# Moving split-matrix sums and modulation-gate sums between the stages of a hybrid attention and mLSTM layer

## The chip, the cores and the metric

The kernel runs on one core of a Trainium2 chip. The metric is device time in microseconds (us) of one execution; times of several executions are given as their median. The engines are TensorE (PE), VectorE (DVE), ScalarE (ACT) and GpSimd (POOL); each works through its own queue in order. SyncE (SP) issues most DMAs, POOL and ACT issue a few. A profile is taken of one execution.

## The reference, cut to what matters

One layer, 256 tokens of width 1024, float32. The input is normalised and modulated by a vector `c`, projected by one wide matrix `w_in` into thirteen parts, sent through a block attention (8 heads) and a chunked mLSTM (4 heads), and the two branches are gated, added and projected out.

```python
ada = c @ w_ada + b_ada
shift, scale, gate = split(ada, 3)
h = rmsnorm(x, norm_w) * (1 + scale) + shift
qa, ka, va, za, qm, km, vm, zm, om, ig, fg, ga, gm = split(h @ w_in)
ya = (attention(rmsnorm(qa), rmsnorm(ka), va) * silu(za)) @ w_att_proj
qm, km = split(silu(causal_dwconv(concat(qm, km))))
hm = rmsnorm(sigmoid(om) * mlstm(qm, km, vm, ig, fg))
ym = (hm * silu(zm)) @ w_ml_proj
y = sigmoid(ga) * ya + sigmoid(gm) * ym
return x + gate * (y @ w_out)
```

`gate` is the last third of `c @ w_ada`: a vector of 1024, used only in the last line. Its weights are 4 MB.

## The kernel before, in words

Float32 products are made of rounded parts. Every matrix is split into a high part (rounded, by ACT: `wh`, line 449) and a low part (the rest, by DVE: `wl`, line 453), and a product is three matmuls: high by high, high by low, low by high. The activations after modulation are kept as `hTh` and `hTl`, transposed.

After a first phase (modulation, normalisation and the first columns of `w_in`, some 52 us) the work is a list of chunks of 512 columns: ka, va, za, qm, zm, km, att (attention projection), vm, ga, om, gm, ml (mixer projection) and out. Each chunk is four steps of PE, so steps are numbered through: za is 12 to 19, qm 20 to 27, zm 28 to 41, km 42 to 49, att 50 to 57, vm 58 to 71, ga 72 to 79, om 80 to 93, gm 94 to 101, ml 102 to 109, out from 110 on. The three chunks zm, vm and om have fourteen steps: they are done as one level of Strassen's scheme with seven products instead of eight. That needs sums of quarters of the weights (`sum_forms`, line 495: tiles t1 and t4 and sums in place, some by an accumulating DMA that POOL issues) and sums of quarters of the activations: `left_sums` (lines 500 to 503 and 510) makes four sums in the tile `lsum`, in two parts, and `left_split` (lines 516 and 517) rounds each on ACT into `Sh` and subtracts on DVE into `Sl`.

The order of everything is written out by hand. At step g the program issues, in this order: for zm, vm and om the evacuation of a finished product; the split of the weights that step g + 4 will use (there are five buffers for `wh` and `wl`); at the first step of a chunk the evacuation of the chunk before; then all hooks that were put at this step with `at(step, ...)`; the weight loads that have become free (six raw buffers); and last the matmuls of the step. `start(name)` is a chunk's first step, `done(name, half)` the one after its last. Each engine executes its share in that order. A hook put at a step thus stands on its engine's queue behind the split for four steps later and ahead of the split of the next step. Steps in the set `pool_lo` have their low part made by POOL instead of DVE; there are six, 26, 27, 49, 50, 53 and 54.

What the change touches:

- `left_sums` at steps 17 and 18, `left_split` at steps 20, 21, 23 and 26.
- The gate vector: `gate_init` brings `c` to all partitions (at step 23 into the third part of the first tile in slot s5, at step 78 again into a tile of its own). `gate_load(q)` loads a quarter of the gate weights, 1 MB, by SP. `gate_acc(j)` multiplies an eighth with `c` and sums it on DVE (line 936, eight of them). `gate_write` and `gate_read` bring the vector by way of DRAM to all partitions, and the output stage multiplies with it (line 956).
- Slots: large tiles share memory under names (s0 to s6, bias). A new tile in a slot waits for the last readers of the tile before. The gate quarters are in s4 (step 23), s5 (step 24), bias (step 88) and s0 (step 99). The tile of the gate vector itself is in s5. `lsum` is in bias, behind the attention's bias table, which the last scores read at step 16.
- `ga_mult` multiplies the sigmoid of ga with the attention branch (line 827), in two halves at steps 77 and 97.
- Around steps 94 to 101 the mLSTM ends: `ml_num` (the numerator, line 875 on DVE), `ml_y` (factors, three small operations on POOL among them, lines 889 to 891), `ml_y2` (scaling, line 900, DVE), `ml_T` (transposes on PE, line 911, then a rounded part `ymh` on ACT, line 915, and a low part `yml` on DVE, line 916). `yh` and `yl` for the output stage are made in `ev_ml` (lines 840 to 843).

Of the kernel before, what the change touches and what calls it, by code (L numbers as in the profile page):

```python
# [9 lines left out]
F32 = mybir.dt.float32  # L10
# [5 lines left out]
D = 1024  # L16
# [48 lines left out]
def tile_hybrid(ctx: ExitStack, tc: tile.TileContext, x, c, params, params2, rel_t, w_row, ada_mod, ada_gate,  # L65
# [136 lines left out]
    cb = ph.tile([128, D], F32, name="cb")  # L202
# [77 lines left out]
    for step in P1_STEPS:  # L280
        op, k = step[0], int(step[1])
# [42 lines left out]
    C, step0, owner = {}, [], []  # L324
# [8 lines left out]
    def start(name, half=0):  # L333
        return step0[C[name, half]]

    def done(name, half):
        return step0[C[name, half]] + (14 if name in STRASSEN else 4)
# [81 lines left out]
    def free(tag):  # L419
        if tag in FREE:  # L420
            hl.tile([128, FREE.pop(tag)], F32, name="free_" + tag, bufs=1)

    def slot(tag, shape, dt, name):
        free(tag)
        return hl.tile(shape, dt, name=name, tag=tag, bufs=1)
# [4 lines left out]
    whl = {}  # L430
    HB = 5
    pool_lo = set()
    for nm, hf in (("qm", 0), ("km", 0), ("km", 1)):
        s = done(nm, hf) + (2 if nm == "qm" else 3)
        pool_lo.update((s, s + 1))
# [22 lines left out]
    def at(step, fn, *a):  # L458
        hooks.setdefault(step, []).append((fn, a))
# [4 lines left out]
    T = {}  # L464
# [49 lines left out]
    def left_split(i):  # L514
        r = T["lsum"][:, (3, 0, 2, 1)[i]]
        nc.scalar.copy(T["Sh"][:, i], r)
        nc.vector.tensor_tensor(T["Sl"][:, i], r, T["Sh"][:, i].bitcast(F32), op=OP.subtract)

    def left(p, k):
# [400 lines left out]
    def gate_init(i):  # L920
        if i == 0:
            T["gcol"] = hl.tile([128, KT], F32, name="gcol")
            T["gw", 1] = slot("s5", [128, 3, D], F32, "gw")
            T["cb"] = T["gw", 1][:, 2]
        else:
            T["cb"] = hl.tile([128, D], F32, name="cbg", tag="NM", bufs=1)
        nc.scalar.dma_start(T["cb"], bass.AP(tensor=c.tensor, offset=c.offset, ap=[[0, 128], [1, D]]))

    def gate_load(q):
        if q != 1:  # L930
            T["gw", q] = slot(("s4", None, "bias", "s0")[q], [128, 2, D], F32, "gw")
        nc.sync.dma_start(T["gw", q][:, 0:2], ada_gate[:, 2 * q:2 * q + 2])

    def gate_acc(j):
# [7 lines left out]

    def gate_read():
        gd = T["gd"]
        T["gateb"] = slot("s5", [128, D], F32, "gateb")
        nc.sync.dma_start(T["gateb"], bass.AP(tensor=gd.tensor, offset=gd.offset, ap=[[0, 128], [1, D]]))

    def load_x():
# [52 lines left out]
    at(s + 4, ml_scores, 2)  # L1001
    at(s + 4, ml_scores, 3)
    at(start("qm") + 3, gate_init, 0)
    at(start("om") - 2, gate_init, 1)
    at(done("ga", 0) + 1, ga_mult, 0)
    at(start("gm") + 3, ga_mult, 1)
    for q, (nm, i, j, k) in enumerate((("qm", 3, 6, 7), ("qm", 4, 23, 25), ("gm", -6, 2, 5), ("ml", -3, 1, 3))):
        s = start(nm)
        at(s + i, gate_load, q)
        at(s + j, gate_acc, 2 * q)  # L1010
        at(s + k, gate_acc, 2 * q + 1)
    at(start("ml") + 5, gate_write)
    at(start("ml") + 7, gate_read)
    at(start("qm") - 3, left_sums, 0)
    at(start("qm") - 2, left_sums, 1)
    for i in range(4):
        at(start("qm") + (0, 1, 3, 6)[i], left_split, i)
    for nm in STRASSEN:
        s = start(nm)
        for p in (3, 4, 5):  # L1020
# [45 lines left out]
    for g in range(NG):  # L1066
# [36 lines left out]
        if ch["kind"] == "str":  # L1103
            p = kp // 2
            o = mmt[ci][(0, 2, 0, 1, 0, 2, 0)[p]]
            for kk in range(2):
                k = 2 * (kp % 2) + kk
# [5 lines left out]
        for kk in range(2):  # L1113
            k = 2 * kp + kk
# [75 lines left out]
```

## Time and profile before

| | |
|---|---|
| median of 3 runs | 358.18 us (357.94 to 358.29) |
| the profiled execution | 357.32 us, of it 355.5 us span |
| mean granted PE clock | 0.993 |
| PE busy | 345.3 us, 97% |
| DVE busy | 293.0 us, 82% |
| ACT busy | 236.4 us, 66% |
| POOL busy | 78.4 us, 22% |
| HBM read | 81.89 MB, 234 GB/s over the span |

Busy shares are means over the whole span. PE's busy time counts matmuls from a modelled start to a modelled end, so it is not a measure of how much work PE could still take; where it waits is seen in the timeline, in which each row gives the start, the length, the engine, the line, the operation, the tiles (written <- read), the shapes, and in brackets the idle time of the engine before it and who ended that.

### The profile page before, as it was taken

The page shows a single profiled execution, that of the slowest core. Times are in us where ns is not written, and L with a number is a line of the kernel's source. Part 1 is how long each engine was busy: PE and PEld are TensorE (multiplying, and loading weights), DVE is VectorE, ACT ScalarE, POOL GpSimd, SP SyncE. Part 2 cuts the span into 40 slices and gives each one's busy share as a digit, 9 for nine tenths or more (in the row PEclk, how much of TensorE's full clock was granted, in tenths as well). Part 3 has the DMA queues.
Part 4 walks back from the last instruction along what each step waited for, and adds up shares of the span by engine and source line. Part 5 has one row for each costly group of instructions (what it writes and reads, how often), then busy time and mean ns, then how long its engine had stood idle before and what let it go on. Part 6 is the DMA issues. An engine that isn't in the chain of part 4 may idle for free.

```text
span 355.5 us, 6025 instructions
## 1 busy us (share of the span) xinstructions
PE 345.3 (97%) x2308; PEld 315.4 (89%) x2308; DVE 293.0 (82%) x423; ACT 236.4 (66%) x366; POOL 78.4 (22%) x88
## 2 busy tenths in 40 slices
PE   8999999999999999799999999999999999999995
PEld 4988889888999999577999998899988998999885
DVE  4899986898958949999986888998988879698772
ACT  3777797989784895778664647884587744654410
POOL 4920004685004356000145250000100014000000
PEclk9999999999999999899999999999999999999998
DMA  8999999994666789956660892929959486065011
GB/s 292 418 418 420 414 372 359 223 269 183 238 207 216 119 307 362 214 206 267 220 254 5 271 287 37 365 104 320 270 167 393 147 278 261 2 235 180 0 61 59
DMA packets 29534, 83.72 MB, mean 235 GB/s; under 512 B 2109, under 2 KB 5185, under 8 KB 28994
## 3 DMA queue, kind: packets, MB, share of 16 engines
q1 hardware_dynamic: 26944, 78.08, 61.6%
q0 software_dynamic: 2112, 4.19, 6.9%
q10 hardware_dynamic: 450, 1.07, 0.9%
q8 instruction: 18, 0.29, 0.3%
q14 instruction: 10, 0.08, 0.1%
HBM read 81.89 MB, written 1.45 MB: 234 GB/s over the span
## 4 chain that ended last, share of the span: by engine, by line
PE 83%; DVE 11%; issue 3%; ACT 1%; DMA 0%; POOL 0%; POOLq 0%; DVEq 0%
PE mm L1127 12%; PE mm L1129 12%; PE mm L1130 12%; PE pm L186 9%; DVE wl L453 6%; PE aux L1109 4%; PE aux L1111 4%; PE aux L1110 4%; PE mm L1120 4%; PE mm L1122 4%; PE mm L1121 4%; PE pg L186 2%; PE xps L244 2%; DVE gw L936 1%; DVE qmT L787 1%
## 5 line engine op out<-in xcount | busy, mean ns | idle before, releaser
L453 DVE TENSOR_TENSOR wl<-raw,wh 128x1024 fp32r<-128x1024 f32 (+1 forms) x100 | 121.1, 1235 | 20.9 <-ACT wh L449 20.8
L449 ACT CAST wh<-raw 128x1024 fp32r<-128x1024 f32 (+1 forms) x106 | 107.2, 1031 | 21.0 <-PE mm L1129 18.4
L1127 PE MATMUL mm<-hTh,wh 128*128 128x256 f32 x320 | 90.4, 282 | 0.2 <-DVE qmT L787 0.2
L1130 PE MATMUL mm<-hTh,wl 128*128 128x256 f32 x320 | 89.5, 280 | 0.0
L1129 PE MATMUL mm<-hTl,wh 128*128 128x256 f32 x320 | 89.5, 280 | 0.0
L1127 PEld LDWEIGHTS mm<-hTh,wh 128*128 128x128 f32 x320 | 60.3, 189 | 0.4 <-issue 0.3
L1129 PEld LDWEIGHTS mm<-hTl,wh 128*128 128x128 f32 x320 | 60.6, 189 | 0.1
L1130 PEld LDWEIGHTS mm<-hTh,wl 128*128 128x128 f32 x320 | 60.3, 188 | 0.0
L453 POOL TENSOR_TENSOR wl<-raw,wh 128x1024 fp32r<-128x1024 f32 x6 | 15.3, 2558 | 55.8 <-ACT wh L449 44.8
L1120 PE MATMUL mm<-wh,hTh 128*128 128x512 f32 (+1 forms) x64 | 23.8, 372 | 0.0
L1122 PE MATMUL mm<-wh,hTl 128*128 128x512 f32 (+1 forms) x64 | 23.2, 363 | 0.0
L1121 PE MATMUL mm<-wl,hTh 128*128 128x512 f32 (+1 forms) x64 | 23.2, 363 | 0.0
L1110 PE MATMUL aux<-wl,Sh 128*128 128x512 f32 x48 | 19.5, 407 | 3.0 <-DVE wl L453 3.0
L1111 PE MATMUL aux<-wh,Sl 128*128 128x512 f32 x48 | 19.2, 400 | 0.0
L1109 PE MATMUL aux<-wh,Sh 128*128 128x512 f32 x48 | 19.2, 400 | 0.0
L175 DVE TENSOR_TENSOR wrl<-raw,wrh 128x512 fp32r<-128x512 f32 (+1 forms) x24 | 18.0, 773 | 1.1 <-ACT wrh L170 0.9
L1129 PE MATMUL mm<-yml,wh 128*128 128x256 f32 x64 | 17.8, 278 | 0.3 <-DVE yml L916 0.3
L449 ACT CAST wh<-t 128x1024 fp32r<-128x1024 f32 x12 | 12.7, 1055 | 8.1 <-PE mm L1129 5.1
L1127 PE MATMUL mm<-yah,wh 128*128 128x256 f32 x64 | 17.8, 279 | 0.0
L1130 PE MATMUL mm<-ymh,wl 128*128 128x256 f32 x64 | 17.7, 276 | 0.0
L1129 PE MATMUL mm<-yal,wh 128*128 128x256 f32 x64 | 17.7, 276 | 0.0
L1127 PE MATMUL mm<-ymh,wh 128*128 128x256 f32 x64 | 17.7, 276 | 0.0
(243 smaller groups left out, 813.4 us busy)
## 6 DMA issues: line engine op xcount, KB each, us to landing
raw<-in_w_in_dram SPq DMA_DIRECT2D x36, 1024.0 KB, 5.1
adat<-in_ada_mod_dram SPq DMA_DIRECT2D x16, 512.0 KB, 9.4
gw<-in_ada_gate_dram SPq DMA_DIRECT2D x4, 1024.0 KB, 7.0
raw<-in_w_att_proj_dram SPq DMA_DIRECT2D x4, 1024.0 KB, 5.4
raw<-in_w_ml_proj_dram SPq DMA_DIRECT2D x4, 1024.0 KB, 4.9
raw<-in_w_out_dram SPq DMA_DIRECT2D x4, 1024.0 KB, 5.5
raw<-in_w_row_dram SPq DMA_DIRECT2D x4, 896.0 KB, 11.8
raw<-in_w_in_dram POOLq DMA_DIRECT2D x3, 1024.0 KB, 12.5
```

The source lines that it names most:

```text
L186: nc.tensor.matmul(pm[ch][:, t], a[:, k, t * 128:(t + 1) * 128], b[:, cs], start=k == 0 and i == 0 and (ch < 3 or t == 0), stop=k == KT - ...
L449: nc.scalar.copy(h, w)
L453: e.tensor_tensor(l, w, h.bitcast(F32), op=OP.subtract)
L1109: nc.tensor.matmul(o, a, wh[:, kk], start=k == 0 and p in (0, 1, 3), stop=False, skip_group_check=True)
L1110: nc.tensor.matmul(o, a, wl[:, kk], start=False, stop=False, skip_group_check=True)
L1111: nc.tensor.matmul(o, b, wh[:, kk], start=False, stop=k == 3, skip_group_check=True)
L1120: nc.tensor.matmul(o, a, wh[:, kk], start=first, stop=False)
L1121: nc.tensor.matmul(o, a, wl[:, kk], start=False, stop=False)
L1122: nc.tensor.matmul(o, b, wh[:, kk], start=False, stop=last)
L1127: nc.tensor.matmul(o, wh[:, kk, cs], sh_[:, k], start=first and i % 2 == 0, stop=False, skip_group_check=True)
L1129: nc.tensor.matmul(o, wh[:, kk, cs], sl_[:, k], start=False, stop=False, skip_group_check=True)
L1130: nc.tensor.matmul(o, wl[:, kk, cs], sh_[:, k], start=False, stop=last and i % 2 == 1, skip_group_check=True)
```

## The change

Three things move.

1. The left sums. `left_sums` goes from steps 17 and 18 to 16 and 17. `left_split` is cut into the rounding on ACT (`left_split`, now at steps 19, 20, 21 and 22) and the subtraction on DVE (`left_low`, at steps 20, 21, 22 and 23).
2. The gate sums. The first quarter is loaded at step 24 into s5 and summed at steps 43 and 45; before, two quarters were loaded at 23 and 24 and summed at 26, 27, 43 and 45. The others are loaded at 88 (bias), 98 (s0) and 99 (s5) and summed at 100 to 105; before, at 88 and 99, summed at 96, 99, 103 and 105. The vector is written at step 106 instead of 107, and its row goes into bias instead of s5. The second `ga_mult` goes from step 97 to 99.
3. The low parts of steps 103 and 104, in the mixer projection, are made by POOL.

```diff
     pool_lo = set()
+    pool_lo.update((step0[C["ml", 0]] + 1, step0[C["ml", 0]] + 2))
...
     def left_split(i):
         r = T["lsum"][:, (3, 0, 2, 1)[i]]
         nc.scalar.copy(T["Sh"][:, i], r)
+
+    def left_low(i):
+        r = T["lsum"][:, (3, 0, 2, 1)[i]]
         nc.vector.tensor_tensor(T["Sl"][:, i], r, T["Sh"][:, i].bitcast(F32), op=OP.subtract)
...
-            T["gw", 1] = slot("s5", [128, 3, D], F32, "gw")
-            T["cb"] = T["gw", 1][:, 2]
+            T["gw", 0] = slot("s5", [128, 3, D], F32, "gw")
+            T["cb"] = T["gw", 0][:, 2]
...
-        if q != 1:
-            T["gw", q] = slot(("s4", None, "bias", "s0")[q], [128, 2, D], F32, "gw")
+        if q:
+            T["gw", q] = slot((None, "bias", "s0", "s5")[q], [128, 2, D], F32, "gw")
...
-        T["gateb"] = slot("s5", [128, D], F32, "gateb")
+        T["gateb"] = slot("bias", [128, D], F32, "gateb")
...
-    at(start("gm") + 3, ga_mult, 1)
-    for q, (nm, i, j, k) in enumerate((("qm", 3, 6, 7), ("qm", 4, 23, 25), ("gm", -6, 2, 5), ("ml", -3, 1, 3))):
+    at(start("gm") + 5, ga_mult, 1)
+    for q, (nm, i, j, k) in enumerate((("km", -18, 1, 3), ("gm", -6, 6, 7), ("ml", -4, 0, 1), ("ml", -3, 2, 3))):
         s = start(nm)
         at(s + i, gate_load, q)
         at(s + j, gate_acc, 2 * q)
         at(s + k, gate_acc, 2 * q + 1)
-    at(start("ml") + 5, gate_write)
+    at(start("ml") + 4, gate_write)
     at(start("ml") + 7, gate_read)
-    at(start("qm") - 3, left_sums, 0)
-    at(start("qm") - 2, left_sums, 1)
+    at(start("qm") - 4, left_sums, 0)
+    at(start("qm") - 3, left_sums, 1)
     for i in range(4):
-        at(start("qm") + (0, 1, 3, 6)[i], left_split, i)
+        at(start("qm") + (-1, 0, 1, 2)[i], left_split, i)
+        at(start("qm") + (0, 1, 2, 3)[i], left_low, i)
```

## The prediction

> **What bounds the kernel now.** I read the page first (busy time, chain, groups), then busy time by stage, then the waits of TensorE (PE) one by one, and last the timelines of VectorE (DVE), ScalarE (ACT) and GpSimd (POOL) around them.
>
> ```profile
> span 355.5 us, 6025 instructions
> ...
> PE 83%; DVE 11%; issue 3%; ACT 1%; DMA 0%; POOL 0%; POOLq 0%; DVEq 0%
> ...
> L453 DVE TENSOR_TENSOR wl<-raw,wh 128x1024 fp32r<-128x1024 f32 (+1 forms) x100 | 121.1, 1235 | 20.9 <-ACT wh L449 20.8
> ...
> gw<-in_ada_gate_dram SPq DMA_DIRECT2D x4, 1024.0 KB, 7.0
> ...
> raw<-in_w_in_dram POOLq DMA_DIRECT2D x3, 1024.0 KB, 12.5
> ```
>
> PE carries 83% of the chain, DVE 11%. The chain names DVE only where PE runs dry, so the next view is by stage (columns: stretch, length, busy time and count of PE, weight load, DVE, ACT, POOL, then granted clock, DMA share, GB/s).
>
> ```profile
> 146.00:148.00 2.00, 0.85 (x4) 0.38 (x2) 2.00 (x4) 2.00 (x4) 0.00 (x0) 1.00 1.11 197
> ...
> 150.00:152.00 2.00, 2.00 (x6) 1.20 (x4) 2.00 (x4) 0.19 (x1) 0.00 (x0) 0.50 0.02 3
> ...
> 154.00:164.00 10.00, 9.72 (x43) 7.70 (x41) 10.00 (x10) 8.16 (x9) 0.00 (x0) 1.00 0.92 340
> 164.00:179.00 15.00, 14.58 (x110) 13.96 (x111) 15.00 (x24) 10.55 (x15) 2.24 (x1) 1.00 0.62 216
> 179.00:285.00 106.00, 106.00 (x744) 98.99 (x743) 90.17 (x102) 71.44 (x92) 15.86 (x11) 1.00 0.66 217
> ```
>
> In these rows up to 179 us DVE is busy all the time (the two stretches left out read the same) and PE is not: that is the zm stage (steps 28 to 41) and the keys. From 179 to 285 PE is never idle. Where PE stands, each row gives the wait before it and who ended it:
>
> ```profile
> 149.28 0.80 PE L1110 MATMUL aux<-wl,Sh 128*128 128x512 f32 x1 [2.43 <-DVE wl L453]
> ...
> 152.75 0.50 PE L1110 MATMUL aux<-wl,Sh 128*128 128x512 f32 x1 [0.55 <-DVE wl L453]
> ...
> 164.26 0.47 PE L1109 MATMUL aux<-wh,hTh 128*128 128x512 f32 x1 [0.54 <-DVE pq L540]
> ...
> 178.13 0.28 PE L1129 MATMUL mm<-hTl,wh 128*128 128x256 f32 x1
> 178.25 0.28 PE L1130 MATMUL mm<-hTh,wl 128*128 128x256 f32 x1
> 178.69 0.36 PE L1127 MATMUL mm<-hTh,wh 128*128 128x256 f32 x1 [0.16 <-DVE qmT L787]
> ...
> 295.74 0.28 PE L1130 MATMUL mm<-hTh,wl 128*128 128x256 f32 x1
> 296.23 0.30 PE L911 MATMUL aux<-ident,omt 128*128 128x128 f32 x1 [0.20 <-ACT wh L449]
> 296.93 0.98 PE L911 MATMUL aux<-ident,omt 128*128 128x128 f32 x7 [0.40 <-DVE omt L900]
> ...
> 306.80 0.28 PE L1130 MATMUL mm<-hTh,wl 128*128 128x256 f32 x1
> 306.91 0.28 PE L1127 MATMUL mm<-ymh,wh 128*128 128x256 f32 x1
> 307.48 0.39 PE L1129 MATMUL mm<-yml,wh 128*128 128x256 f32 x1 [0.29 <-DVE yml L916]
> ```
>
> Four waits stand in the DVE-bound stretch, two more places at 296 to 307 us, where the normalised mLSTM output is transposed and split. All but the 0.20 at 296.23 end with DVE. So an edit is worth what it takes off DVE's queue ahead of these places.
>
> **The change, part by part.** First the stretch ahead of 149.28:
>
> ```profile
> 107.62 0.17 DVE L729 RECIPROCAL st<-st 128x2 f32<-128x2 f32 x1 [3.52 <-ACT P L724]
> ...
> 110.44 3.99 DVE L510 TENSOR_TENSOR lsum<-hTh,hTl 128x512 f32<-128x512 f32 x4
> ...
> 131.78 1.15 DVE L517 TENSOR_TENSOR Sl<-lsum,Sh 128x512 fp32r<-128x512 f32 x1 [2.16 <-ACT Sh L516]
> 132.85 2.31 DVE L453 TENSOR_TENSOR wl<-raw,wh 128x1024 fp32r<-128x1024 f32 x1
> ...
> 145.06 1.27 DVE L936 CUSTOM_DVE_ANT_0 gw<-gw,prm 128x1024 f32<-128x1024 f32 x1
> ...
> 146.27 0.68 DVE L517 TENSOR_TENSOR Sl<-lsum,Sh 128x512 fp32r<-128x512 f32 x1
> 146.87 1.22 DVE L495 TENSOR_TENSOR t<-raw 128x1024 f32<-128x1024 f32 x1
> 148.01 1.22 DVE L453 TENSOR_TENSOR wl<-t,wh 128x1024 fp32r<-128x1024 f32 x1
> 149.14 1.28 DVE L936 CUSTOM_DVE_ANT_0 gw<-gw,prm 128x1024 f32<-128x1024 f32 x1
> ...
> 150.34 1.22 DVE L495 TENSOR_TENSOR t<-raw 128x1024 f32<-128x1024 f32 x1
> ...
> 131.65 1.05 ACT L449 CAST wh<-raw 128x1024 fp32r<-128x1024 f32 x1
> ```
>
> (1) Left sums one step sooner. The first four adds (3.99 us) fall into DVE's wait of 3.52 us before 107.62, where POOL is idle; without POOL beside them an add of this shape takes about 0.68 (the Sl row at 146.27), so 4 x 0.68 = 2.7 fits. The four subtractions of the second part move into the place at 110.44. Cost nothing; if the cover went, DVE would do them where it does now, which is also nothing.
>
> (2) Low parts a step behind their rounding. The ACT copies go to steps 19 to 22, the DVE subtractions to 20 to 23. ACT does four copies ahead of step 28's cast instead of three; it loses a wait for DVE of about the same length, so I leave that cast at 131.65 and step 28's low part at 132.85. Behind the moved copies ACT holds casts for steps that PE reaches 10 us later. DVE no longer stands 2.16 us behind a copy just issued, and the last Sl leaves the full stretch: 146.87 - 146.27 = 0.60 us.
>
> (3) The first two gate sums leave steps 26 and 27: 146.27 - 145.06 = 1.21 and 150.34 - 149.14 = 1.20 us. At the keys (steps 43 and 45) two sums stand before and after, with other numbers. The load into s4 at step 23 goes with them: one issue less on SP's queue, 1 MB less traffic; the load into s5 at step 24 keeps its place.
>
> DVE has no gap from there to 178.69, so 0.60 + 1.21 + 1.20 = **3.0 us** pass through. Step by step: the low part of step 31 ends at 149.23 - 1.81 = 147.4, that of step 32, which released PE at 152.75, at 149.7, the evacuation before 164.26 at 161.3, and the one that frees step 46's bank at 175.7. PE waits again at each, for less. Next late is still DVE. The accumulating load that POOL issues for the zm stage takes 12.5 us to land, at about 150, where DMA stops (3 GB/s from 150 to 152); the low part that needs it comes up on DVE at 153, the cast it needs ends at 151.7, so 1.4 us of cover remain and I price it at nothing. Bounds: 2.4 (the Sl stays in the way) to 4.0 (step 28's low part, 2.31 here against the group's mean of 1.24 because POOL works beside it, starts cleaner). I take 3.0, the rows themselves.
>
> (4) The later sums, the product with the attention branch and POOL's two low parts:
>
> ```profile
> 289.56 1.28 DVE L936 CUSTOM_DVE_ANT_0 gw<-gw,cbg,prm 128x1024 f32<-128x1024 f32 x1
> ...
> 292.59 1.22 DVE L827 TENSOR_TENSOR gat<-gat,attT 128x1024 f32<-128x1024 f32 x1
> ...
> 295.60 1.66 DVE L900 SCALAR_TENSOR_TENSOR omt<-omt,f,zmt 128x256 f32<-128x256 f32 x4
> ...
> 320.70 0.68 DVE L840 TENSOR_TENSOR yf<-mm,gmt 128x512 f32<-128x512 f32 x1
> ...
> 300.27 0.47 ACT L915 ACTIVATE ymh<-aux,prm 128x256 fp32r<-128x256 f32 x1 [2.27 <-DVE omt L900]
> ...
> 128.72 2.40 POOL L453 TENSOR_TENSOR wl<-raw,wh 128x1024 fp32r<-128x1024 f32 x1 [9.88 <-PE mm L1130]
> ...
> 134.04 3.39 POOL L453 TENSOR_TENSOR wl<-raw,wh 128x1024 fp32r<-128x1024 f32 x1
> ```
>
> The sum at 289.56 and the product at 292.59 lie ahead of the scaling at 295.60 that PE's transposes wait for. Without them (1.2 and 1.1 us) the scaling starts well over a microsecond sooner and what PE loses between 295.74 and 296.93 goes (1.19 us for two matmuls that need 0.12 each, so 0.95, of which I take 0.9); ymh follows the second scaling, which comes sooner by the same, so the 0.46 at 307.48 (0.57 less the usual 0.11) goes too: at most 1.35. Against it, DVE now has six sums and the product from step 99 to 105, and POOL two low parts (2 x 2.40, due at PE four steps or 4 x 2.72 = 10.9 us later, so hidden; on POOL they stand behind the small factors of the scaling, and nothing waits behind them). DVE's own sum is even: two sums more (2 x 1.28) for two low parts less (2 x 1.22). Per step a sum and a low part are 2.4 us against PE's 2.72 (24 matmuls at 0.113), so it keeps up, and what waited at 320.70 starts near 319.5. But POOL runs beside the second scaling, the product and one sum, all with two SBUF operands. Bounds from the 132.85 row: none, or each DVE operation under POOL's 4.8 us at half speed, 2.4 us. At 2.4 DVE reaches 320.70's work 1.2 late and the output stage waits for it: gain nothing. At about 1.0, where I put it since the split of yml reads PSUM, the gain is **1.0 us**.
>
> The Trainium skill, "GPSIMD Engine Reference", section "8. Key points", says that GpSimd shares its SBUF interfaces with VectorE and contends with VectorE instructions that read two SBUF inputs. The trace agrees: 2.31 against 1.24 us for the same split. Taken as full exclusion it is the slower rival below.
>
> (5) The loads at steps 98 and 99 (s0, s5) stand on SP beside those of w_out; their first sums come four steps later, a load of this kind lands in 7.0, so nothing. gate_write a step sooner and the row read into bias: nothing, its row is used at 340.
>
> Sum: 3.0 + 1.0 = 4.0 us. The profiled execution's 357.32 (355.5 of span and 1.8 around it) becomes 353.3; it ran 0.86 below the median of 358.18, so I forecast **354.2** for the median.
>
> **The rivals.**
> (a) The later stage gives nothing, as the half-speed bound has it: 358.18 - 3.0 = 355.2. For it: 132.85. Against: yml and the scores read PSUM.
> (b) The sooner sums do nothing (DVE or ACT holds them as before), so the Sl stays in the full stretch: 354.8, inside the forecast's range. Against: the 3.52 us wait.
> (c) PE's own pace. A step of 256 columns runs at two paces: 0.118 us a matmul at 178.13 to 178.25 and 0.113 before 306.91, with no wait between; 24 x 0.005 is 0.11 us a step. The quick pace follows the waits at 178.69 and 307. If fewer waits leave it slow through the 22 steps behind them it costs 2.4: 356.6, and with (a) 357.6, no measurable change. Nothing tells what sets it.
> (d) Slower: POOL and DVE exclude each other at the mixer projection. POOL's two low parts at 3.39 each, with DVE standing all that time, put DVE 6.8 us back; the output stage, which starts from DVE's split of y, ends 6.8 - 2.3 = 4.5 later, against 3.0 gained: 359.7. It decides from 3.0 + 2.3 = 5.3 us on. Against: only part of DVE's work there has two SBUF operands, and under POOL the split took 2.31, not 1.24 + 3.39.
> (e) Better: the clean start of step 28 (1.0) and all of the later 1.35: 352.8.
>
> **How the numbers follow.** Forecast with (b), 353.3 to 355.0: 0.57. (a): 0.15. (c): 0.13, of it 0.05 without measurable change. (d): 0.08. (e): 0.07. This kernel's runs spread over 0.35 us, so 0.2% (0.7 us) is what can be told from no change. Faster: 0.57 + 0.15 + 0.08 + 0.07 = 0.87; same 0.05; slower 0.08. The range runs from (e) to (c): 352.8 to 356.6, leaving out (d) and the worst of (c), 0.13.
>
> **What would show it.** Right: between the split of step 28 and 150 us no gate sum and no Sl on DVE; the 2.43 us wait below 1 us; step 46 about 3 us sooner; no wait of PE at the transposes after the om stage; POOL's low parts ending before PE needs them. Wrong: DVE idle between 140 and 179 (another engine bounds), step 28's low part later than 132.9, DVE operations at 297 to 306 stretched by more than 2.4 in sum, or PE waiting for yl in the output stage.

## The result, and the profile after

The changed kernel takes 355.94 us (median of 7 runs, 354.53 to 356.98) against 358.35 us of the kernel before measured beside it (7 runs, 357.94 to 359.49). The ratio is 0.9917, 95% interval 0.9893 to 0.9942. The profiled execution took 354.78 us, of it 353.0 us span, 2.54 less than the profiled execution of before.

First the page of the changed kernel: span, chain by engine, and the groups that answer to those shown of before.

```profile
span 353.0 us, 6025 instructions
...
PE 67%; DMA 12%; DVE 9%; POOL 4%; ACT 4%; issue 3%; SPq 0%; DVEq 0%; ACTq 0%; POOLq 0%
...
L454 DVE TENSOR_TENSOR wl<-raw,wh 128x1024 fp32r<-128x1024 f32 (+1 forms) x98 | 118.4, 1233 | 23.5 <-ACT wh L450 23.4
...
L1115 PE MATMUL aux<-wl,Sh 128*128 128x512 f32 x48 | 19.2, 399 | 1.2 <-DVE wl L454 1.2
```

DVE makes two low parts less (98), and PE now waits 1.2 us in all for the low parts of the Strassen products. The share that the chain gives to DMA does not belong to the change: the first phase was followed back another way there. Line numbers are one to five higher than before.

The stage view (columns as before), first a row of the kernel before, then the changed kernel and the waits of PE in it:

```profile
148.00:150.00 2.00, 0.72 (x2) 0.64 (x3) 2.00 (x3) 1.33 (x2) 0.00 (x0) 0.71 1.07 195
```

```profile
146.00:148.00 2.00, 1.41 (x7) 0.83 (x6) 2.00 (x3) 2.00 (x4) 0.00 (x0) 1.00 1.06 211
148.00:150.00 2.00, 1.38 (x7) 0.82 (x6) 2.00 (x3) 1.32 (x2) 0.00 (x0) 1.00 1.13 207
150.00:152.00 2.00, 2.00 (x10) 1.63 (x9) 2.00 (x3) 0.62 (x1) 0.00 (x0) 1.00 0.58 89
```

```profile
147.38 0.50 PE L1115 MATMUL aux<-wl,Sh 128*128 128x512 f32 x1 [0.59 <-DVE wl L454]
...
149.65 0.50 PE L1115 MATMUL aux<-wl,Sh 128*128 128x512 f32 x1 [0.62 <-DVE wl L454]
...
161.16 0.47 PE L1114 MATMUL aux<-wh,hTh 128*128 128x512 f32 x1 [0.36 <-DVE pq L544]
...
175.59 0.36 PE L1132 MATMUL mm<-hTh,wh 128*128 128x256 f32 x1
```

PE still stands four times (the last is seen only from the starts: the matmul before it starts at 175.17) and DVE is still busy all the time, but the first stop, 2.43 us before, is 0.59, the second is 0.62 instead of 0.55, and the granted clock, 0.71 and 0.50 in the two rows from 148 to 152 before, stays at 1.00.

Where the time then goes is seen best by the start of a step's first matmul, against the same step of the kernel before (us; negative is sooner; one profiled execution each):

| kernel | 28 | 46 | 58 | 94 | 99 | 103 | 110 | 113 |
|---|---|---|---|---|---|---|---|---|
| after | +0.15 | -3.10 | -3.11 | -2.47 | -3.48 | -3.77 | -3.02 | -2.59 |
| after, second profile | -0.13 | -3.34 | -2.10 | -1.47 | -2.48 | -2.76 | -2.02 | -1.59 |
| former addresses | -0.02 | -3.27 | -3.28 | -3.28 | -4.30 | -4.58 | -3.84 | -3.40 |
| second ga_mult at 84 | -0.13 | -3.34 | -2.10 | -1.31 | -2.29 | -2.57 | -2.58 | -2.01 |
| both of these | -0.10 | -3.35 | -3.35 | -2.99 | -3.90 | -4.23 | -4.23 | -3.72 |
| both, second profile | +0.08 | -3.16 | -3.16 | -2.77 | -3.75 | -3.76 | -3.01 | -3.01 |
| left sums alone | +0.05 | +0.15 | +0.14 | +0.14 | +0.14 | +0.20 | +0.95 | +0.95 |
| gate sums alone | -0.14 | -2.55 | -1.31 | -1.31 | -2.33 | -2.46 | -2.46 | -1.18 |
| both, without POOL | +0.20 | -3.03 | -1.79 | -1.44 | -2.39 | -2.67 | -1.93 | -1.93 |
| four sums early | +0.99 | -2.25 | -2.26 | -2.26 | -3.27 | -3.40 | -3.40 | -3.40 |

The first row is the account of the change: 3.10 gained up to step 46, 0.63 lost between 58 and 94, 1.01 gained at the transposes before 99, 0.48 at 103 less 0.19 lost in between, 0.75 lost up to 110 and 0.43 in the output stage: 2.59, nearly the 2.5 of the span. Step 28, the first of the zm stage, lies ahead of what the gate sums can speed up, and within 0.2 us of the kernel before (0.99 in the last row). Counted from there, every kernel of the table that has both parts gains 3.21 to 3.25 up to step 46, and the gate sums alone gain 2.41.

### The profile page after: what moved, and what is told of

It reads as the page before. It is cut to its first block, busy times and chain, and to the rows that moved or that the text cites. A ratio compares the mean times of both kernels' runs of the same rounds, so it can differ in the third digit from the quotient of the medians.

```text
span 353.0 us, 6025 instructions
## 1 busy us (share of the span) xinstructions
PE 345.2 (98%) x2308; PEld 313.9 (89%) x2308; DVE 290.2 (82%) x421; ACT 236.1 (67%) x366; POOL 85.0 (24%) x90
## 4 chain that ended last, share of the span: by engine, by line
PE 67%; DMA 12%; DVE 9%; POOL 4%; ACT 4%; issue 3%; SPq 0%; DVEq 0%; ACTq 0%; POOLq 0%
PE mm L1132 14%; PE mm L1134 14%; PE mm L1135 14%; DMA raw<-in_w_row_dram 12%; DVE wl L454 5%; PE aux L1115 4%; PE aux L1114 4%; PE aux L1116 4%; POOL ms L592 3%; PE mm L1127 1%; PE mm L1125 1%; PE mm L1126 1%; DVE qmT L791 1%; POOL ms L591 1%; PE mm L1146 1%
## 5 line engine op out<-in xcount | busy, mean ns | idle before, releaser
L454 DVE TENSOR_TENSOR wl<-raw,wh 128x1024 fp32r<-128x1024 f32 (+1 forms) x98 | 118.4, 1233 | 23.5 <-ACT wh L450 23.4
L454 POOL TENSOR_TENSOR wl<-raw,wh 128x1024 fp32r<-128x1024 f32 x8 | 19.7, 2465 | 58.9 <-ACT wh L450 47.2
L170 ACT CAST wrh<-raw 128x512 fp32r<-128x512 f32 (+1 forms) x24 | 15.8, 687 | 3.7 <-DMA raw<-in_w_row_dram 3.6
```

The source lines that it names most:

```text
L454: e.tensor_tensor(l, w, h.bitcast(F32), op=OP.subtract)
```

## The experiments

**The same kernel again.** Does the profile of the changed kernel repeat?

> The changed kernel again, unaltered, to see what differs between two profiles of one program. If PE's pace in the 256-column steps (113 or 118 ns a matmul) and in the Strassen products of Sh and Sl (227 or 234 ns) belongs to the program (addresses, order), it is 118 from step 94 to 109 and 234 in those products again, and the time is within 0.5 us of 354.8. If the pace is a matter of chance in each execution, steps 100 to 109 may come out at 113 and the time is 353.5 to 357.

Measured: 355.76 us (354.68 to 356.31), ratio 0.9909 (0.9877 to 0.9941). The second profile is 1.0 us longer than the first. It is 0.24 ahead at step 46 and then loses 1.24 up to step 58: those twelve steps ran at 118 ns a matmul, in the first profile at 113, with the same instructions in the same order. So the two paces that the prediction saw do not belong to the place in the program alone, and they make the 1 us between these two profiles.

**Addresses.** In the changed kernel `Sh` and `Sl` are allocated a step sooner, ahead of other tiles, and so lie 6432 bytes lower. This kernel allocates them in the second part of `left_sums`, at the addresses of before; the instructions are those of the changed kernel.

```diff
     def left_sums(part):
         if part:
             r = T["lsum"]
+            Sh = ...; Sl = ...; T["Sh"], T["Sl"] = Sh, Sl
...
         r = slot("bias", [128, 4, 4, 128], F32, "lsum")
-        Sh = ...; Sl = ...
```

> The tiles Sh and Sl are made one hook later, behind those of the mLSTM gates, so that they get the addresses that they had before the change (6432 bytes higher); no instruction moves. Theory 1, the address sets the pace of the Strassen products that load weights from Sh and Sl: 234 goes back to 227 ns a matmul in 16 steps of vm and om (0.64 us) and in zm (there DVE is the bound, so nothing), 0.6 us faster than the changed kernel. Theory 2, the pace comes from the order or is chance: 234 ns stays, no change.

Measured: 356.02 us (353.93 to 356.75), ratio 0.9907 (0.9871 to 0.9944); profiled execution 353.93. The groups by line and shape in a stretch of vm, first of the changed kernel, then of this one, tell it apart:

```profile
L1114 PE MATMUL aux<-wh,Sh 128*128 128x512 f32 x8 | 3.2, 395 | 0.0
L1115 PE MATMUL aux<-wl,Sh 128*128 128x512 f32 x8 | 3.2, 395 | 0.0
L1116 PE MATMUL aux<-wh,Sl 128*128 128x512 f32 x8 | 3.2, 394 | 0.0
```

```profile
L1117 PE MATMUL aux<-wh,Sl 128*128 128x512 f32 x5 | 1.9, 389 | 0.0
L1115 PE MATMUL aux<-wh,Sh 128*128 128x512 f32 x4 | 1.6, 389 | 0.0
L1116 PE MATMUL aux<-wl,Sh 128*128 128x512 f32 x4 | 1.6, 389 | 0.0
```

The third column is the mean of one: 395 ns at the new addresses, 389 at the old ones, as in the kernel before. From start to start it is 234 against 227 ns; six matmuls a step in sixteen such steps of vm and om make 16 x 6 x 0.007 = 0.67 us. In the table the 0.63 between steps 58 and 94 is back (-3.28 at both). The median (356.02 against 355.94 and 355.76) does not show it, and six executions that spread over 2.8 us could hardly do so. It rests on the profiles: these products take 234 ns in all five of this record with the new addresses, and 227 in all eight with the old ones.

**The second ga_mult.** The product of `gat` stands at step 99, where the evacuation of gm's first half, which takes the memory of attention's branch (slot s4), waits for it. ACT, POOL and DVE of the changed kernel there:

```profile
296.67 1.02 ACT L836 ACTIVATE gmt<-mm 128x1024 f32<-128x1024 f32 x1 [4.96 <-DVE gat L831]
297.59 1.04 ACT L450 CAST wh<-raw 128x1024 fp32r<-128x1024 f32 x1
298.52 0.48 ACT L919 ACTIVATE ymh<-aux,prm 128x256 fp32r<-128x256 f32 x1
```

```profile
298.70 2.40 POOL L454 TENSOR_TENSOR wl<-raw,wh 128x1024 fp32r<-128x1024 f32 x1 [4.98 <-ACT wh L450]
```

```profile
293.76 1.68 DVE L904 SCALAR_TENSOR_TENSOR omt<-omt,f,zmt 128x256 f32<-128x256 f32 x4
295.35 1.22 DVE L831 TENSOR_TENSOR gat<-gat,attT 128x1024 f32<-128x1024 f32 x1
299.03 0.48 DVE L920 SCALAR_TENSOR_TENSOR yml<-aux,prm,ymh 128x256 fp32r<-128x256 f32 x1 [2.46 <-ACT ymh L919]
```

ACT stands 4.96 us; behind it wait the cast for POOL's low part, ymh, and so DVE for 2.46. This wait is new, and the prediction does not have it. The experiment takes it away:

```diff
-    at(start("gm") + 5, ga_mult, 1)
+    at(start("om") + 4, ga_mult, 1)
```

> The second ga_mult goes to step 84, ahead of the step at which the tile of gm takes its slot. Theory 1: ACT's wait of 4.96 us before the evacuation of gm goes (it waits for a DVE product two places later in the program), the low parts of the mixer's input start 2 to 3 us sooner, the output stage's first work on DVE starts 2 us or more sooner and PE's 0.4 us loss at step 112 goes: 0.4 us faster than the changed kernel. Rival: the wait is slack that nothing sees, or DVE's 1.2 us in the om stage stalls PE there: no change or up to 0.8 slower.

Measured: 355.90 us (354.89 to 356.83), ratio 0.9915 (0.9884 to 0.9947). The wait of ACT is gone, and another takes its place: POOL now starts its low part while DVE does the second scaling. DVE in this kernel, the first and the second scaling by the same instructions:

```profile
292.25 1.67 DVE L904 SCALAR_TENSOR_TENSOR omt<-omt,f,zmt 128x256 f32<-128x256 f32 x4
...
295.15 3.81 DVE L904 SCALAR_TENSOR_TENSOR omt<-omt,f,zmt 128x256 f32<-128x256 f32 x4
```

1.67 becomes 3.81 us beside POOL (four operations each): the wait on gm's memory had kept POOL out of DVE's way. It had a price all the same. In the changed kernel the low part of y that step 112 needs ends on DVE 2.01 us sooner than in the kernel before (332.40 against 334.41), while step 99 starts 3.48 sooner: between the two DVE falls 1.47 us back. So it does in the second profile and at the former addresses; with the product at step 84 it falls 0.82 back. This profile does not gain by it: the stretched scaling costs PE 0.28 at step 100, steps 100 to 109 ran at 113 ns instead of 118, and PE, so much sooner at the output stage, loses 0.57 there.

**Both.** Former addresses and ga_mult at step 84.

> Both of these edits together. Theory 1 of each: 0.64 + 0.4 = 1.0 us faster than the changed kernel, 353.8 in a run like the first profiled one; if only the place of Sh and Sl counts 0.6, if neither does nothing.

Measured: 355.24 us (353.66 to 355.95), ratio 0.9894 (0.9860 to 0.9928); run again on another occasion 355.25 (354.32 to 356.61), ratio 0.9897 (0.9868 to 0.9927), for which this was expected:

> The kernel with the former addresses and the second ga_mult at step 84, unchanged, beside four_early on the same chip: 355.2 (354 to 356). If the spread of its profiles comes from the two paces alone, its step 46 stands at -3.1 to -3.4 against before, and steps 46 to 57 run at either 113 or 118 ns.

It was the fastest kernel up to then, but its interval overlaps with that of the changed kernel. Its product at step 84 cost 0.27 at step 92 in both profiles, and the scaling was again stretched to 3.81. Steps 46 to 57 ran at 113 ns in both profiles. They differ in steps 101 to 109, which ran at 113 in the first and 118 in the second. DVE falls 0.76 and 0.80 us back from step 99 on, much as with the product at 84 alone; the first profile loses 0.51 in the output stage, the second, in which PE comes 1.2 us later, nothing (-3.01 at 110 and at 113).

**Each part alone.** The left sums on the kernel before (with `Sh` and `Sl` at their old addresses):

> The kernel before with the first part of the change alone (left sums a step sooner, low parts a step behind their rounding), Sh and Sl at the addresses of before; all gate sums where they were. Theory 1, the zm stage gains what leaves DVE's queue: only the one Sl of 0.60 us goes, the start of step 46 comes 0.6 us sooner than before and the time is 357.6 where before has 358.2. Rival, the sooner sums are what frees the stage: 2 to 3 us sooner, 355.5.

Measured: 358.11 us (10 runs, 356.55 to 359.27) against 358.40, ratio 0.9984 (0.9963 to 1.0005): no change that can be told. Step 46 is not sooner. DVE of this kernel, then its stage view:

```profile
148.35 1.27 DVE L940 CUSTOM_DVE_ANT_0 gw<-gw,prm 128x1024 f32<-128x1024 f32 x1
...
150.70 6.88 DVE L453 TENSOR_TENSOR wl<-raw,wh 128x1024 fp32r<-128x1024 f32 x6
158.42 2.36 DVE L453 TENSOR_TENSOR wl<-raw,wh 128x1024 fp32r<-128x1024 f32 x2 [0.84 <-ACT wh L449]
```

```profile
148.00:150.00 2.00, 1.52 (x6) 1.09 (x6) 2.00 (x4) 0.62 (x1) 0.00 (x0) 0.91 1.13 207
150.00:152.00 2.00, 0.52 (x3) 0.04 (x1) 2.00 (x3) 1.30 (x2) 0.00 (x0) 0.50 0.31 55
152.00:154.00 2.00, 2.00 (x5) 1.62 (x6) 2.00 (x2) 0.33 (x1) 0.00 (x0) 0.50 0.00 0
154.00:156.00 2.00, 2.00 (x7) 1.51 (x6) 2.00 (x3) 1.04 (x1) 0.00 (x0) 0.50 0.88 258
```

With the gate sums still in the way PE stood twice,

```profile
148.48 0.50 PE L1115 MATMUL aux<-wl,Sh 128*128 128x512 f32 x1 [1.85 <-DVE wl L453]
...
151.96 0.79 PE L1115 MATMUL aux<-wl,Sh 128*128 128x512 f32 x1 [1.48 <-DVE wl L453]
```

and its clock fell to 0.50 for some 6 us instead of the 3.5 of before. In that time PE itself became the slowest: ACT waited for PE (2.16 us before its cast at 154.50, 1.31 before its copy at 156.85), and DVE, which had been 0.8 us ahead (its second gate sum begins at 148.35 instead of 149.14), stood 0.84 for ACT and had lost it all. The Trainium skill, "TensorE: Matmul & The Clock Gate", section "Part 1: The HAM clock gate", lets the clock fall to half after an idle window of about 3.4 us; in these profiles a single stop of 2.43 us (before) and two of 1.85 and 1.48 were enough, and two of 0.6 were not.

The clock does not fall in every execution, though. Of the ten of this kernel, five have a mean granted clock of 0.998 to 1.000 and a median of 357.64; the other five, the profiled one among them, have 0.988 to 0.990 and 358.58. The kernel before, measured beside it, has 358.28 (4 executions) from 0.998 on and 359.07 (7) up to 0.991. By these medians the left sums alone may well gain 0.5 to 0.6 in either case; with so few executions that is not shown.

The gate sums with their loads, without the left sums, without POOL and with ga_mult at step 97:

> The kernel before with the gate sums and loads of the change alone; the second ga_mult stays at step 97, no low part goes to POOL, the left sums stay. Theory 1: 2.4 us leave DVE's queue ahead of the zm stage, step 46 comes 2.4 us sooner; at the mixer projection DVE has two sums more and gets late, so that the output stage gives 1 to 2 us back: about 357. Rival, the stage needs the sooner left sums too: step 46 less than 1.5 us sooner.

Measured: 356.18 us (354.98 to 356.38), ratio 0.9932 (0.9905 to 0.9958). Step 46 is 2.55 sooner, 2.41 counted from step 28, and 1.21 + 1.20 = 2.41 was the sum for this part. The changed kernel has 3.25 counted so, which leaves 0.84 for the left sums, 0.60 by the prediction. Without the gate sums in the way their gain is there in every profile; beside them it is not there in the one profile taken. The transposes' 1.02 is also here without POOL. The output stage loses 1.28 in this profile, more than with POOL: PE waited there for the rounded part of y (0.71) and for the low part, which DVE reached late behind six gate sums and two low parts more: it falls 1.73 back from step 99 on.

**Without POOL's low parts**, with the former addresses and ga_mult at step 84:

> The version with both edits (Sh and Sl at the old addresses, second ga_mult at step 84), but the low parts of steps 103 and 104 made by DVE again. Theory 1, POOL beside DVE stretches DVE's second scaling from 1.66 to 3.81 us and so gives back what it takes off: the scaling is 1.66 again, DVE makes two low parts more (2.3 us), the output stage starts within 0.5 us of the version with POOL, same time. Rival, POOL's two low parts are worth their 2.3 us: the output stage starts 2 us later, 355.5 in a run where the other has 353.7.

Measured: 355.43 us (355.22 to 355.99), ratio 0.9917 (0.9889 to 0.9945), against 355.24 and 355.25 with POOL. The second scaling took 1.67 here. In the profile of both, the stretch cost PE 0.23 at step 100 (-3.90 to -3.67), which is absent here; but behind that stop steps 101 to 109 ran at 113 ns there, and at 118 here (118 also in the second profile of both, behind the same stop). DVE falls 0.79 back from step 99 on, as with POOL, and the output stage loses nothing. POOL's two low parts are worth nothing that can be measured either way.

**What sets PE's pace.** Two small matmuls with a POOL memset between them make PE stand, at steps 73 and 96:

```diff
+    def probe():
+        x = T["probe"]
+        nc.tensor.matmul(aux([128, 32]), ident, x, start=True, stop=True)
+        nc.gpsimd.memset(x, 0.0)
+        nc.tensor.matmul(aux([128, 32]), ident, x, start=True, stop=True)
```

> The changed kernel with two short waits put into PE's queue, at steps 73 and 96: a matmul of 32 columns, a memset of its operand by POOL, and the matmul again, which computes nothing that is used. Theory 1, a wait of PE that is long enough makes the pace of the 256-column steps quick until something makes it slow again: steps 73 to 79 and 96 to 109 go from 118 to 113 ns a matmul, which gains 0.8 and up to 1.5 us for some 0.8 us that each wait costs. Rival, the pace is chance or belongs to stages: 118 stays in one or both, and the waits cost 1.6 us.

Measured: 363.74 us (362.29 to 364.41), ratio 1.0141 (1.0102 to 1.0181), far more than the waits meant. The second probe was badly placed: its memset lay on POOL's queue behind the factors of the scaling, which waited for DVE, so PE stood for some 6 us at step 96. POOL in this kernel:

```profile
288.80 0.20 POOL L893 TENSOR_SCALAR f<-f 128x4 f32<-128x4 f32 x1 [40.28 <-DVE f L892]
...
290.34 0.11 POOL L1057 MEMSET probe<- 128x32 f32 x1
```

The first probe worked: steps 73 to 79, at 118 ns in every profile without a probe there, went to 113. So the probes were set where POOL is free, at steps 13, 43 and 73:

> The kernel after, with a pair of 32-column matmuls and a POOL memset between them at steps 13, 43 and 73, so that TensorE stands still about 0.5 to 0.9 us in three steps that ran at 118 ns a matmul in all runs so far. Theory (the pace is set anew whenever TensorE has stood still): it goes to 113 ns right behind some of the three probes and stays so up to the next stop. If a stop always gives the quick pace: 113 behind all three. If it depends on the stop's length or phase: behind some. Rival (the pace belongs to the step's operands or place): 118 in all of steps 14 to 19, 44, 45 and 73 to 79. Time: 3 x 0.8 more, less 0.11 per quick step: 356 to 358.

Measured (one run): 355.88 us. PE at the probes of steps 43 and 13:

```profile
168.24 0.41 PE L1058 MATMUL aux<-probe,ident 128*128 128x32 f32 x2 [0.24 <-POOL probe L1057]
```

```profile
91.67 0.41 PE L1058 MATMUL aux<-probe,ident 128*128 128x32 f32 x2 [0.24 <-POOL probe L1057]
```

The stops look alike, but behind step 43 the pace was 113 (steps 43 to 49) and behind step 73 too (73 to 79), while steps 13 to 16 kept 118 (step 17 alone ran at 113). So a stop can set the pace anew, and which it gives is not decided by its length. Three probes cost 3 x 0.8 us and gave 0.11 us a step back. What decides stays open.

**Four sums early.** The changed kernel with former addresses, ga_mult at 97, no POOL, and the second gate quarter summed in km:

```diff
-    for q, ... (("km", -18, 1, 3), ("gm", -6, 6, 7), ("ml", -4, 0, 1), ("ml", -3, 2, 3))
+    for q, ... (("km", -18, 1, 3), ("km", 1, 6, 7), ("gm", -6, 6, 7), ("ml", -3, 1, 3))
```

> The kernel after, with Sh and Sl at their former addresses, without POOL's two low parts, with the second ga_mult back at step 97, and with the second gate quarter loaded at step 43 into the memory of lsum (free from step 24 to 53) and summed at steps 48 and 49, where VectorE stood still 2.98 us; the last stage then has four gate sums instead of six. Theory (the later loss comes from the six sums and from POOL and the gm wait, the 7 ns from the addresses): step 46 3.1 to 3.4 us sooner than before, products with Sh and Sl at 227 ns, step 99 another 1.0 sooner and step 103 0.5, no wait of TensorE at the output's third step; median 354.0 to 354.8. Rival (the number of sums does not matter, the output stage is late for another reason): the third output step loses 0.4 to 0.9 again, median 355.2 to 356. Rival (the sums at 48 and 49 delay the scores): TensorE waits at steps 50 to 53.

Measured: 354.89 us (352.77 to 355.76), ratio 0.9885 (0.9849 to 0.9920). The lowest median of all, just above the band that was expected, and the interval overlaps with those of the changed kernel and of "both" (355.25 beside it), so that it is better is likely and not shown. Its profile had lost 0.8 us at step 10, ahead of everything that was changed, which is why its row of the table stands at -2.25 at step 46; from step 28 it gains 3.24. What the table shows is the end: -3.40 at step 103 and still at 113. DVE of this kernel in km and at the end of ml:

```profile
186.49 1.28 DVE L940 CUSTOM_DVE_ANT_0 gw<-gw,prm 128x1024 f32<-128x1024 f32 x1
...
187.69 3.38 DVE L940 CUSTOM_DVE_ANT_0 gw<-gw,prm 128x1024 f32<-128x1024 f32 x1
...
317.37 0.68 DVE L844 TENSOR_TENSOR yf<-mm,gmt 128x512 f32<-128x512 f32 x1
```

The split of y starts at 317.37 instead of 319.31 in the changed kernel, the output stage does not wait, and the second early sum, stretched to 3.38 beside POOL's low parts of steps 53 and 54, delays nothing. From step 99 on DVE falls not back at all but gains 0.13, where the gate sums alone, which also have the product at 97 and no POOL, fall 1.73 back. So two sums less behind step 99 are enough to end the loss in the output, even at the quick pace. They are not its only cause: with all six sums but the product at step 84 DVE falls back 0.8 instead of 1.47, and then the two profiles at 118 ns (both, second profile, and without POOL) lost nothing there, and the two at 113 lost 0.5 to 0.6.

## Why the prediction was right, and where its sum was too large

The time, 355.94, lies in the range of 352.8 to 356.6 but 1.7 above the 354.2 forecast: 4.0 us were summed and 2.4 came.

- **Step (3), the zm stage, and the 0.60 of step (2)**: right in size, place and cause. 3.0 was summed, 3.10 measured, or 3.25 counted from step 28, where this execution was 0.15 late. PE's four waits were put at 147.4, 149.7, 161.3 and 175.7 and came at 147.38, 149.65, 161.16 and 175.59; that they agree so closely is in part luck, since the 0.15 and the 0.25 more gained nearly cancel. Nearly all of this 0.25 was there ahead of the places of the gate sums: a wait of DVE for ACT, 0.68 us before 140.45 in the kernel before, was gone, which no term of the sum has, and what DVE began at 142.79 it began at 142.71. Two details of step (2) were wrong. DVE still stood 1.82 us behind a copy of ACT, and step 28's low part came at 132.96, past the 132.9 named as a sign of being wrong (in an execution 0.15 late); it took 1.77 instead of 2.31 us, and the sum behind it 2.33 instead of 1.21, both beside POOL. The cover of 1.4 us for the accumulating load was also thinner: ACT stood 1.94 us for it before its cast at 151.38, and DVE had no gap. And the terms do not simply add: with the gate sums in place, the left sums gave nothing in the profile taken (+0.15 at step 46), where the halved clock took over as the bound.
- **Step (1)**: the four adds took 2.49 us in DVE's wait (2.7 estimated) and cost nothing in time. Their tiles did: moving the allocation moved the addresses, and that cost 0.63 in stages that the diff does not touch. The prediction has no term for it. This is the first missing size, shown by the kernel with the former addresses.
- **Step (4)**: the transposes gave 1.01 (0.9 taken), the wait for yml 0.48 (0.46). So the gain itself was all of the 1.35 named as the most, and a little more, not the 1.0 taken. The lag charged to DVE beside POOL was not there, for a reason the prediction missed: ACT's 4.96 us wait for the product moved POOL's low parts behind the scaling. Where that wait was taken away the stretch came, 2.14 us, within the 0 to 2.4 that were its bounds. The rule of the Trainium skill quoted there (contention with VectorE instructions of two SBUF inputs) agrees with 1.67 against 3.81. But what PE lost behind it, 0.94 by its pace and 0.43 in the output, left 0.12 of these 1.49: step 94 is 2.47 sooner and step 113 2.59. So the term of 1.0 was right in its gains and far too large as a sum.
- **PE waiting for yl in the output stage**, listed as what would show the prediction wrong, came. PE's first matmul of the low part starts at 332.45, and the low part ends on DVE at 331.71 + 0.69 = 332.40:

```profile
331.71 0.69 DVE L847 TENSOR_TENSOR hTl<-yf,hTh 128x512 fp32r<-128x512 f32 x1 [0.69 <-ACT hTh L846]
```

```profile
332.45 0.50 PE L1127 MATMUL mm<-wh,hTl 128*128 128x512 f32 x1
```

It cost 0.43. The prediction had DVE's work even (two sums more for two low parts less) and what waited at 320.70 starting near 319.5; it started at 319.31, but PE came 3 us sooner. That comparison was left out, and so was the wait for the product at step 99, which holds DVE up by some 0.65 us (it falls 1.47 back with it and 0.82 without).
- **Rival (c), PE's pace**, was right, and in part or whole it is what came. Its 22 steps are 46 to 57 and 100 to 109. In the first profile the former kept 113, and the latter, in which PE no longer stood at the transposes, stayed at 118; in the second profile, whose 355.74 is nearer to the median, all 22 ran at 118. Groups of the mixer projection, of the kernel after and of the kernel before (third column the mean of one):

```profile
L1135 PE MATMUL mm<-ymh,wl 128*128 128x256 f32 x64 | 18.0, 281 | 0.0
```

```profile
L1127 PE MATMUL mm<-ymh,wh 128*128 128x256 f32 x64 | 17.7, 276 | 0.0
```

The 5 ns a matmul made 0.75 + 0.19 = 0.94 us. With 24 x 0.005 = 0.11 a step the price was right, and it belonged into the sum with some weight. That the edit itself slows these steps, by removing a stop behind which the quick pace can begin, is argued and not shown: in the kernel before, step 99, right behind the stop, still ran at 118 and only step 100 at 113. How many of the 22 steps were struck is chance: the second profile lost 1.24 in steps 46 to 57 as well.

The mechanisms of rivals (a) and (b) are refuted by the steps themselves (transposes 1.01 sooner, Sl out of the full stretch), though the later stage gave next to nothing in sum, as (a) has it, and its 355.2 is nearer to 355.94 than the forecast; (d), the slowdown through POOL, did not come: even the 3.81 us scaling cost PE 0.23.

So the missing 1.6 of the sum is, by the profiles, 0.63 of addresses, 0.94 of pace and 0.43 of output, less 0.59 by which the two gains were larger than summed (1.49 instead of 1.0, 3.10 instead of 3.0): 1.4 of the profiles' 1.5. The rest lies between profiles and medians. Each size is from one profile of each kernel; the addresses and the output are the same in the second profile, and the pace cost more there.

## What to carry to other kernels

When a helper engine's queue is full in a stretch, work taken off it there can come back one for one (2.41 summed and measured), and the place of the next waits can be given to some 0.1 us; but follow the bound engine to the end of the kernel, since coming 3 us sooner makes work late there that was in time. Compare the addresses of tiles too when an allocation moves, and the mean duration of the main groups before and after, not only the waits. Before a wait is removed, see whom it keeps apart: here a wait of 5 us on one engine was what kept two others from slowing each other down.

## What the runs showed of the hardware that was not expected

- The same 128x512 matmul takes 234 instead of 227 ns from start to start when `Sh` and `Sl` are allocated sooner and so lie 6432 bytes lower; three products of a step alike. Why these addresses, no run here shows.
- Steps of 128x256 matmuls run at 113 or 118 ns, and either holds through many steps. In the probes a new pace began at a stop of PE; two like stops gave different paces, and the same program had either in two executions. It makes up to 1.2 us between two profiles of one program, more than some edits are worth.
- In the profiles the granted clock fell to 0.50 for 3.5 us after a stop of 2.43 us, and for 6 us after stops of 1.85 and 1.48; with stops of 0.6 it stayed at 1.00. The same program need not do so each time: of 38 executions of the kernel before whose mean granted clock is on record, 15 have 0.998 to 1.000 and 17 have 0.988 to 0.991.
- POOL's subtraction beside DVE stretched four DVE operations with two SBUF operands from 1.67 to 3.81 us, and a gate sum from 1.28 to 3.38. POOL's own operation took 2.44 to 2.49 instead of 2.40 in the first case, and two together 6.16 in the second.
